# Adaptive average pooling in one dimension: the final scaling moves from ScalarE to GpSimd

## The chip, the cores and the metric

The kernel runs on one core of a Trainium2 chip. The metric is the device time of one execution in microseconds; the time before is the median of three runs. The engines are named as the profile names them: DVE (VectorE), ACT (ScalarE), POOL (GpSimd), PE (TensorE, unused here) and SP (SyncE, which issues the DMAs here). SPq and POOLq are the instruction queues of SP and POOL.

## What is computed

The input x is float32 of shape 32 x 256 x 4096. Each row of 4096 values is cut into 256 windows of 16, and the output is the mean of each window:

```python
for i in range(output_size):            # output_size = 256
    start = int(i * length / output_size)
    end = int((i + 1) * length / output_size)
    result[:, :, i] = np.mean(x[:, :, start:end], axis=-1)
```

134.2 MB are read and 8.4 MB are written; there is one addition for each value read.

## The kernel before

The 32 x 256 = 8192 rows are worked through in 16 tiles of 512 rows, four rows (R) on each of the 128 partitions. A tile `xin` thus has 1024 cells (windows) of 16 values per partition, 8.39 MB in all. The pool `inpool` has two buffers, so tile t + 2 can be loaded when tile t has been read for the last time.

For each tile, in this order in the text:

- SP issues the load (line 74).
- POOL takes the second half of the cells (512 of 1024) and adds the last eight values of each window onto the first eight, in place (line 77). That is an operation of 4096 elements per partition with two inputs.
- DVE sums the 16 values of each cell of the first half into the result (line 82, 8192 elements per partition), and needs only the load for it.
- DVE sums the eight remaining values of each cell of the second half (line 85, 4096 elements per partition), and waits for POOL's add.
- ACT multiplies the tile's 1024 results by 1/16, in place (line 88), and waits for line 85.

The results stay in the core's memory: those of the first 14 tiles in `res_many`, those of the last two in `res_few`. They leave in two stores, which SP issues as well through the function `store` (its DMA is line 61): `res_many` (7.34 MB) is issued once the last load has been issued, in the loop's last turn, and waits for the scaling of tile 13; `res_few` (1.05 MB) is issued after the loop and waits for the scaling of tile 15. Both stores wait in SP's queue in the order of the text, so a load that stands ahead of them is issued first.

Tile, the layer in which the kernel is written, sets the semaphores between the engines; each engine runs its instructions in the order of the text. At the end line 97 and what follows join the engines, and SP waits until both stores have landed (line 99). Line 116 stands for a preamble that fills four constants on POOL; line 130 for the entry into the program.

Of the kernel before, what the change touches and what calls it, by code (L numbers as in the profile page):

```python
# [1 line left out]

# [4 lines left out]


@with_exitstack
def kernel(  # L10
    ctx: ExitStack,
    tc: tile.TileContext,
    x: bass.AP,
    output_size: int,
    out: bass.AP,
):

    nc = tc.nc
    F32 = mybir.dt.float32
    X = mybir.AxisListType.X

    batch, channels, length = x.shape
    ob, oc, olen = out.shape
    assert ob == batch and oc == channels and olen == output_size
    assert length % output_size == 0
    window = length // output_size  # L30
    hw = window // 2
    inv_w = 1.0 / float(window)

    P = nc.NUM_PARTITIONS
    R = 4
    tail = 2
    rows = batch * channels
    assert rows % (P * R) == 0
    ntiles = rows // (P * R)
    head = ntiles - tail  # L40
    many = head * R
    few = tail * R
    cells = R * output_size
    m = cells // 2
    cols = R * length

    xr = x.rearrange("b c l -> (b c) l")
    orow = out.rearrange("b c o -> (b c) o")
    x_many = xr[0 : P * many, :].rearrange("(p r) l -> p (r l)", p=P, r=many)
    o_many = orow[0 : P * many, :].rearrange("(p r) o -> p (r o)", p=P, r=many)  # L50
    x_few = xr[P * many :, :].rearrange("(p r) l -> p (r l)", p=P, r=few)
    o_few = orow[P * many :, :].rearrange("(p r) o -> p (r o)", p=P, r=few)

    res_many = nc.alloc_sbuf_tensor("res_many", [P, head * cells], F32, align_bytes=256)
    res_few = nc.alloc_sbuf_tensor("res_few", [P, tail * cells], F32, align_bytes=256)
    inpool = ctx.enter_context(tc.tile_pool(name="inpool", bufs=2))

    stored = nc.alloc_semaphore("stored")

    def store(out, in_):  # L60
        ins = nc.sync.dma_start(out=out, in_=in_)
        tc.no_tile_sem_insts.add(ins.ins.name)
        ins.then_inc(stored, 16)

    for t in range(ntiles):
        k = t - head
        xin = inpool.tile([P, cells, window], F32, name="xin")
        if k < 0:
            res, base = res_many, t * cells
            src = x_many[:, t * cols : (t + 1) * cols]  # L70
        else:
            res, base = res_few, k * cells
            src = x_few[:, k * cols : (k + 1) * cols]
        nc.sync.dma_start(out=xin.rearrange("p o w -> p (o w)"), in_=src)  # L74
        if t == ntiles - 1:
            store(o_many, res_many[:, :])
        nc.gpsimd.tensor_add(  # L77
            out=xin[:, m:cells, 0:hw],
            in0=xin[:, m:cells, 0:hw],
            in1=xin[:, m:cells, hw:window],  # L80
        )
        nc.vector.reduce_sum(  # L82
            out=res[:, base : base + m], in_=xin[:, 0:m, :], axis=X
        )
        nc.vector.reduce_sum(  # L85
            out=res[:, base + m : base + cells], in_=xin[:, m:cells, 0:hw], axis=X
        )
        nc.scalar.mul(  # L88
            out=res[:, base : base + cells],
            in_=res[:, base : base + cells],  # L90
            mul=inv_w,
        )
    store(o_few, res_few[:, :])

    ctx.pop_all().close()
    tc.close()
    tc.compile()  # L97
    nc.sync.wait_ge(stored, 32)
    nc.sync.sem_clear(stored)


# [1 line left out]
_INS = ['x', 'output_size']  # L103
_OUTS = [((32, 256, 256), 'float32')]

_NUMBERS = {'output_size': 256}


# [26 lines left out]
```

## Time and profile before

| | |
|---|---|
| median of three runs | 333.5 us (333.26 to 333.58) |
| profiled execution | 333.14 us, of which the span in the profile 331.8 us |
| DVE busy | 209.7 us, 63% of the span, 32 instructions |
| POOL busy | 139.7 us, 42%, 20 instructions |
| ACT busy | 18.2 us, 5%, 17 instructions (16 scalings of 1.056 us, one table load of 1.283 us) |
| POOL's add, line 77 | 16 of 8.717 us |
| DVE's sums, lines 82 and 85 | 16 of 8.686 us and 16 of 4.420 us |
| DMA | 142.61 MB, mean 430 GB/s |

The span runs from the first to the last thing that the profile shows of the program. Busy times are those of instructions at work, without waits. In the profile's lists an operation reads "engine line operation output<-input (partitions x elements)". In the timeline the first column is the start in microseconds from the span's start, the second the duration, and the brackets hold how long the engine had been idle and what ended that. In lists of waits, "a <- b: total, times, longest" says that a waited for b.

### The profile page before, as it was taken

How to read it: one execution, taken by the hardware profiler on the slowest of the kernel's cores; microseconds unless marked ns; L12 is line 12 of the kernel's file. 1: busy time of each engine (PE TensorE's matmuls, PEld its weight loads, DVE VectorE, ACT ScalarE, POOL GpSimd, SP SyncE). 2: the span in 40 equal slices, each digit the busy share in tenths (PEclk: the TensorE clock that was granted, in tenths of full speed). 3: DMA queues.
4: the chain of work that ended last, by engine and by line, in shares of the span. 5: the costliest groups of instructions: out<-in, count | busy, mean ns of one | idle time of the engine just before them, and what ended most of it. 6: DMA issues, size and time to landing. Idle time of an engine off the chain costs nothing.

```text
span 331.8 us, 159 instructions
## 1 busy us (share of the span) xinstructions
DVE 209.7 (63%) x32; ACT 18.2 (5%) x17; POOL 139.7 (42%) x20
## 2 busy tenths in 40 slices
DVE  0029396692939669392966939295693929569392
ACT  1000101001010100001010000101000010100001
POOL 0027090642709164270906437090643709063370
DMA  9898989989898998989899898989899898989998
GB/s 379 379 506 379 506 379 411 474 379 506 379 506 379 427 458 379 506 379 506 379 458 427 379 506 379 506 379 498 387 403 482 379 506 379 506 379 442 411 442 348
DMA packets 2592, 142.61 MB, mean 430 GB/s; under 512 B 288, under 2 KB 288, under 8 KB 288
## 3 DMA queue, kind: packets, MB, share of 16 engines
q1 hardware_dynamic: 2592, 142.61, 99.4%
HBM read 134.22 MB, written 8.39 MB: 430 GB/s over the span
## 4 chain that ended last, share of the span: by engine, by line
DMA 66%; POOL 18%; DVE 11%; POOLq 3%; issue 0%; ACT 0%; SPq 0%
DMA xin<-in_x_dram 66%; POOL xin L77 18%; DVE res_many L85 9%; POOLq L97 3%; DVE res_few L85 1%; ACT res_few L88 0%; SPq L74 0%; POOLq L77 0%
## 5 line engine op out<-in xcount | busy, mean ns | idle before, releaser
L77 POOL TENSOR_TENSOR xin<-xin 128x4096 f32<-128x4096 f32 x16 | 139.5, 8717 | 181.4 <-DMA xin<-in_x_dram 181.4
L82 DVE TENSOR_REDUCE res_many<-xin 128x512 f32<-128x8192 f32 x14 | 121.6, 8686 | 101.3 <-DMA xin<-in_x_dram 101.3
L85 DVE TENSOR_REDUCE res_many<-xin 128x512 f32<-128x4096 f32 x14 | 61.9, 4420 | 2.3 <-POOL xin L77 2.1
L88 ACT ACTIVATE res_many<-res_many 128x1024 f32<-128x1024 f32 x14 | 14.8, 1056 | 271.3 <-DVE res_many L85 271.3
L82 DVE TENSOR_REDUCE res_few<-xin 128x512 f32<-128x8192 f32 x2 | 17.4, 8686 | 12.1 <-DMA xin<-in_x_dram 12.1
L85 DVE TENSOR_REDUCE res_few<-xin 128x512 f32<-128x4096 f32 x2 | 8.8, 4420 | 0.3 <-POOL xin L77 0.3
L88 ACT ACTIVATE res_few<-res_few 128x1024 f32<-128x1024 f32 x2 | 2.1, 1056 | 36.6 <-DVE res_few L85 36.6
L88 ACT ACT_TABLE_LOAD x1 | 1.3, 1283 | 0.7 <-PEq L116 0.7
L116 POOL MEMSET const-float32-0.0<- 128x1 f32 x1 | 0.1, 98 | 0.2 <-issue 0.2
L116 POOL MEMSET const-uint8-127<- 128x1 uint8 x1 | 0.1, 102 | 0.0
L116 POOL MEMSET const-bfloat16-1.0<- 128x1 bf16 x1 | 0.1, 101 | 0.0
L116 POOL MEMSET const-float32-1.0<- 128x1 f32 x1 | 0.1, 99 | 0.0
## 6 DMA issues: line engine op xcount, KB each, us to landing
out_dram<-res_many SPq DMA_DIRECT2D x1, 7168.0 KB, 41.2
out_dram<-res_few SPq DMA_DIRECT2D x1, 1024.0 KB, 4.9
xin<-in_x_dram SPq DMA_DIRECT2D x16, 25.4
```

What stands on the lines that cost most here:

```text
L77: nc.gpsimd.tensor_add(out=xin[:, m:cells, 0:hw], in0=xin[:, m:cells, 0:hw], in1=xin[:, m:cells, hw:window],)
L82: nc.vector.reduce_sum(out=res[:, base : base + m], in_=xin[:, 0:m, :], axis=X)
L85: nc.vector.reduce_sum(out=res[:, base + m : base + cells], in_=xin[:, m:cells, 0:hw], axis=X)
L88: nc.scalar.mul(out=res[:, base : base + cells], in_=res[:, base : base + cells], mul=inv_w,)
L97: tc.compile()
L116: nc = _bacc.Bacc("TRN2", target_bir_lowering=False, num_devices=1)
```

## The change

POOL multiplies each tile's 1024 results by 1/16 instead of ACT. The operation, its operands and its place in the text stay the same. ACT is left with no instruction of the kernel, and the table load ahead of its first one goes too.

```diff
-        nc.scalar.mul(
+        nc.gpsimd.tensor_scalar_mul(
             out=res[:, base : base + cells],
-            in_=res[:, base : base + cells],
-            mul=inv_w,
+            in0=res[:, base : base + cells],
+            scalar1=inv_w,
         )
```

In the built program POOL's instructions then stand in the order add (tile 0), scale (0), add (1), scale (1) and so on; those of DVE and SP stand as before. The two stores wait for POOL where they waited for ACT, and from the third tile on the add waits for its load and for POOL's own scaling two tiles before, where it waited for its load and for DVE.

## The prediction

> **What bounds the kernel now.** I read the page's slices and queue table first, then the timeline of the last tiles, then the waits of the DMA queue's own engine, and last the tail in windows of 0.1 us. The slices and the queue table:
>
> ```profile
> DMA  9898989989898998989899898989899898989998
> ...
> q1 hardware_dynamic: 2592, 142.61, 99.4%
> HBM read 134.22 MB, written 8.39 MB: 430 GB/s over the span
> ```
>
> One queue is at work for 99.4% of 16 engines' span, and no slice is below eight tenths. All traffic (16 loads of 8.39 MB, stores of 7.34 and 1.05 MB) goes through it one after the other. The timeline of the last two tiles, SP's issues among the engines' work:
>
> ```profile
> 282.64 4.42 DVE L85 TENSOR_REDUCE res_many<-xin 128x512 f32<-128x4096 f32 x1 [0.17 <-POOL xin L77]
> 287.09 0.33 SPq L74 DMA_DIRECT2D xin<-in_x_dram  x1
> 287.10 1.06 ACT L88 ACTIVATE res_many<-res_many 128x1024 f32<-128x1024 f32 x1 [18.23 <-DVE res_many L85]
> 288.18 0.35 SPq L61 DMA_DIRECT2D out_dram<-res_many  x1
> 293.09 8.69 DVE L82 TENSOR_REDUCE res_few<-xin 128x512 f32<-128x8192 f32 x1 [6.03 <-DMA xin<-in_x_dram]
> 293.20 8.72 POOL L77 TENSOR_TENSOR xin<-xin 128x4096 f32<-128x4096 f32 x1 [10.59 <-DMA xin<-in_x_dram]
> ...
> 312.47 8.69 DVE L82 TENSOR_REDUCE res_few<-xin 128x512 f32<-128x8192 f32 x1 [6.10 <-DMA xin<-in_x_dram]
> 312.58 8.72 POOL L77 TENSOR_TENSOR xin<-xin 128x4096 f32<-128x4096 f32 x1 [10.66 <-DMA xin<-in_x_dram]
> 321.33 4.42 DVE L85 TENSOR_REDUCE res_few<-xin 128x512 f32<-128x4096 f32 x1 [0.17 <-POOL xin L77]
> 325.78 1.06 ACT L88 ACTIVATE res_few<-res_few 128x1024 f32<-128x1024 f32 x1 [18.32 <-DVE res_few L85]
> 326.86 0.34 SPq L61 DMA_DIRECT2D out_dram<-res_few  x1
> ```
>
> A tile takes 312.47 - 293.09 = 19.38 us, and its bytes need that: 8.39 MB / 19.38 us = 433 GB/s. Its buffer is free when L85 ends (287.06); SP hands over the load after next at 287.09, while the load in flight lands only at 293.08. So 6.0 us of transfer are queued at each handover, and the queue does not run dry. The queue's own waits say which engine SP depends on:
>
> ```profile
> SPq L74 <- DVE res_many L85: 185.8, 14, 13.3
> ...
> SPq L61 <- ACT res_few L88: 38.3, 1, 38.3
> SPq L61 <- ACT res_many L88: 0.7, 1, 0.7
> ```
>
> The loads wait for DVE and for earlier loads; the scaling is awaited by the two stores alone. The chain of waits gives DMA 66%, POOL 18% and DVE 11%, but it follows each buffer's reuse and does not see that the other buffer's load runs meanwhile, so I do not price by it. What remains is the tail, where a store seems to wait for the last scaling. In windows of 0.1 us (bounds, length, busy time of DVE, ACT and POOL, clock, DMA share, GB/s):
>
> ```profile
> 326.50:326.60 0.10, 0.00 (x0) 0.10 (x1) 0.00 (x0) 1.00 3.97 1720
> ...
> 326.80:326.90 0.10, 0.00 (x0) 0.04 (x1) 0.00 (x0) 1.00 1.32 573
> 326.90:327.00 0.10, 0.00 (x0) 0.00 (x0) 0.00 (x0) 1.00 0.00 0
> ...
> 328.60:328.70 0.10, 0.00 (x0) 0.00 (x0) 0.00 (x0) 1.00 0.60 246
> ```
>
> A packet is counted whole where it starts: shares above 1 show it, and so does the first load, issued at 0.74, whose 65 KB packets already appear from 1.70 on. So the last 16 packets of the big store (57 KB each) start at 326.5 to 326.9. The row of 326.50 holds three of them with 3.97 x 0.1 us x 16 engines / 3 = 2.12 us each: the engines are busy until 328.62 to 329.0. The first packet of the small store starts at 328.6. The end is thus set by bytes too, and the last scaling has some cover.
>
> **The change part by part.** Removed: ACT's table load (1.28 us, 0.74 to 2.02) and 16 scalings of 1.056 us. ACT's first scaling starts at 35.75, so nothing waits for the table; cost of the removal 0, hidden by the first load. The instruction order of the changed build has POOL alternate add and scale, with DVE's and SP's instructions as before; the stores now wait for POOL.
>
> Added: 16 scalings of 128x1024 on POOL, an operation that the trace does not show there. Nearest rows: POOL's four start-up fills of one element take 0.10 us, which I take as the fixed cost; the add takes 8.717 us for 4096 outputs, (8717 - 100) / 4096 = 2.10 ns per element with two reads and a write. The scaling has one read and one write. High bound: it goes at the add's rate, 0.10 + 1024 x 2.10 ns = 2.25 us. Low bound: the add's time is its three streams in turn, and the scaling overlaps its two: a third of it, 0.10 + 0.72 = 0.82 us. I take 1.2 us (half the add's rate, 0.10 + 1.08, the reads in turn), which is near DVE's one-input rate (4420 / 4096 = 1.08 ns per element) and ACT's (1.03).
>
> The Trainium skill ("GPSIMD Engine Reference", 4.1 Engine selection, and 3.1) advises against elementwise work on GpSimd, as about twice as slow as VectorE for two inputs, but calls one input roughly line rate, and gives 1.03 cycles per element for the lightest loops; the add here agrees with its two-input figure of 2.6 cycles at 1.2 GHz (8717 ns / 4096 x 1.2 = 2.55). By that page the scaling is 1024 x 1.03 / 1.2 = 0.88 us, an estimate, and the sum below stays as it is.
>
> Where POOL starts after a signal: for the same landing it starts 0.11 us after DVE (312.58 against 312.47), so the scaling starts 0 to 0.11 us later than ACT's did.
>
> In the steady state: the next add is now queued on POOL behind the scaling, which waits for L85. For tile 13 the scaling would run from about 287.2 to 288.4; the add behind it starts at 293.20, when its load lands. So 4.8 us are spare (3.8 at 2.25 us). Behind the add stand L85 of the next tile and, behind that, SP's load; they are late only if the scaling takes over 6.0 us. The adds' wait for DVE becomes one for POOL's own scaling of two tiles before, long done. DVE idles while POOL scales, so no overlap of the two is added; cost 0. Were the cover gone, it would be the scaling's 1.2 us for each of 15 tiles, 18 us.
>
> The big store's issue moves from 288.18 to about 288.4 (289.5 at the high bound), but its first packet starts at 311.7, behind the load handed over at 287.09: 22 us of cover, cost 0.
>
> The tail: the last scaling starts at 325.78 to 325.89 and ends at 327.07 (chosen), so the small store is issued at 327.09 instead of 326.86, 0.23 us later (bounds: 0.24 earlier, 1.30 later). From issue to first packet the first load took 0.96 us, eleven of its 16 packets started by 1.36 us, and the last at 2.06 us. Issued at 326.86, the small store could have begun at 327.8 to 328.2, and the engines came free from 328.6: cover of 0.4 to 0.8 us, by the slowest packets none. The chosen 0.23 us lies inside: cost 0. At the high bound 1.30 - (0.4 to 0.8) = 0.5 to 0.9 us show; without cover 1.3 us. An earlier issue gains nothing, as the bytes ahead of it stay.
>
> **The sum:** 331.8 us span + 0, and 333.14 - 331.8 = 1.34 us around it: 333.14 us. The profiled execution is 0.36 below the median of the runs, 333.5, so I give 333.5.
>
> **The rivals.**
> (1) *The last scaling sticks out of the cover*: it costs as much per element as the add. For: POOL's only wide operation runs at that rate. Against: it has one read fewer. Time 333.5 + 0.5 to 0.9 = 334.0 to 334.4.
> (2) *Slower: a scaling that is slow by itself*, say at twice the add's rate, 4.4 us. It ends at 330.3, the small store's packets start 0.96 to 1.36 us later, at 331.2 to 331.6 instead of 328.6: 2.6 to 3.0 us, 336.1 to 336.5. It decides from about 2.3 us on, where the tail's loss passes 0.67 us. For: the operation's price on POOL is not in the trace. Against: no row of any engine is that slow per element.
> (3) *POOL becomes the bound*: a scaling over 5.9 us makes add, reduce and scaling longer than the 19.38 us of a load. At 8.7 us a tile takes 8.7 + 4.4 + 8.7 + 0.3 = 22.1 us, and from 22.55 on 16 of them end at 376; with store and launch about 382. It needs four times the add's rate.
> (4) *Faster: the table load held up the start.* It runs at 0.74 to 2.02, and five of the 16 first packets start at 2.2 to 2.8, after eleven by 2.1. Were these five released, up to 0.7 us would go: 332.8 to 333.3. Against: the late packets are shorter (2.8 us against 3.1), and the rate over all later windows is 437 GB/s whatever the stagger.
>
> **How the numbers follow.** Forecast (hidden) 0.60; (1) 0.17; (2) 0.11; (3) 0.03; (4) 0.09. A measurement of this kernel can tell about 0.2% (0.67 us) from no change. Of (1) a third passes it, of (4) half. Slower: 0.05 + 0.11 + 0.03 = 0.19. Faster: 0.05. Same: 0.76. The range: the forecast and the spread of the runs (333.26 to 333.58), down to 332.9 for most of (4), and up to 335.0, which holds (1), its case without cover (334.8), and the start of (2): about 0.87 of the chance.
>
> **What would show it.** POOL rows of line 88, 128x1024, near 1.2 us; the adds still released by the load and not by POOL's queue; SP's store of the small result released by POOL at about 327.1; its first packets still near 328.6, and no gap after the big store's last ones; tiles still 19.38 us apart. I am wrong if the scaling takes over 2.3 us, if the small store's packets start more than 0.7 us later than before, or if the tiles' spacing moves. If the first packets bunch by 2.1 us with the table load gone and the whole tail comes earlier, (4) is right.

## The result, and the profile after

The changed kernel takes 334.14 us (median of 10 runs, 333.82 to 334.6) against 333.4 us (10 runs, 333.26 to 333.58) for the kernel before: a ratio of 1.0024, 95% interval 1.0015 to 1.0032, so it is 0.7 us slower. The profiled execution took 334.06 us with a span of 332.6 us (before 333.14 and 331.8).

The page of the changed kernel, its queue table and POOL's groups (busy time and mean duration, then the idle time before and what ended it):

```profile
q1 hardware_dynamic: 2592, 142.61, 99.2%
...
L77 POOL TENSOR_TENSOR xin<-xin 128x4096 f32<-128x4096 f32 x16 | 139.5, 8717 | 71.9 <-DMA xin<-in_x_dram 71.9
L88 POOL TENSOR_SCALAR res_many<-res_many 128x1024 f32<-128x1024 f32 x14 | 38.7, 2768 | 63.6 <-DVE res_many L85 63.6
...
L88 POOL TENSOR_SCALAR res_few<-res_few 128x1024 f32<-128x1024 f32 x2 | 5.5, 2768 | 9.1 <-DVE res_few L85 9.1
```

The scaling takes 2.768 us on POOL, 2.6 times ACT's 1.056. The adds are as long as before and still end their waits on the load. The last two tiles in the changed kernel's timeline:

```profile
293.28 8.69 DVE L82 TENSOR_REDUCE res_few<-xin 128x512 f32<-128x8192 f32 x1 [6.09 <-DMA xin<-in_x_dram]
293.40 8.72 POOL L77 TENSOR_TENSOR xin<-xin 128x4096 f32<-128x4096 f32 x1 [3.35 <-DMA xin<-in_x_dram]
...
312.58 8.69 DVE L82 TENSOR_REDUCE res_few<-xin 128x512 f32<-128x8192 f32 x1 [6.02 <-DMA xin<-in_x_dram]
312.70 8.72 POOL L77 TENSOR_TENSOR xin<-xin 128x4096 f32<-128x4096 f32 x1 [3.28 <-DMA xin<-in_x_dram]
321.45 4.42 DVE L85 TENSOR_REDUCE res_few<-xin 128x512 f32<-128x4096 f32 x1 [0.18 <-POOL xin L77]
325.96 2.77 POOL L88 TENSOR_SCALAR res_few<-res_few 128x1024 f32<-128x1024 f32 x1 [4.54 <-DVE res_few L85]
328.75 0.34 SPq L61 DMA_DIRECT2D out_dram<-res_few  x1
```

Up to the last sum nothing has changed: the tiles are 312.58 - 293.28 = 19.30 us apart (19.38 before; over all tiles 19.32 and 19.33), POOL still idles 3.3 us before each of these adds, and tile 15 lands 0.11 us later than before. Then the last scaling runs to 328.73, and the small store is issued at 328.75 instead of 326.86. The tail in windows of 0.1 us (bounds, length, busy time of DVE and POOL, clock, DMA share, GB/s):

```profile
326.50:326.60 0.10, 0.00 (x0) 0.10 (x1) 1.00 3.97 1720
...
327.00:327.10 0.10, 0.00 (x0) 0.10 (x1) 1.00 2.65 1147
327.10:327.20 0.10, 0.00 (x0) 0.10 (x1) 1.00 0.00 0
...
329.50:329.60 0.10, 0.00 (x0) 0.00 (x0) 1.00 0.19 82
329.60:329.70 0.10, 0.00 (x0) 0.00 (x0) 1.00 2.30 983
```

The last packets of the big store start at 326.5 to 327.1 and take 2.12 us each, so the engines come free at 328.6 to 329.2. The small store's first packet starts at 329.5, where it started at 328.6 before. So the queue now runs dry for some 0.3 to 0.9 us, once, at the end.

### The profile page after: what moved, and what is told of

Read it like the earlier page. It is cut to its first block, busy times and chain, and to the rows that moved or that the text cites. A ratio compares the mean times of both kernels' runs of the same rounds, so it can differ in the third digit from the quotient of the medians.

```text
span 332.6 us, 158 instructions
## 1 busy us (share of the span) xinstructions
DVE 209.7 (63%) x32; POOL 183.9 (55%) x36
## 4 chain that ended last, share of the span: by engine, by line
DMA 66%; POOL 21%; DVE 9%; issue 2%; POOLq 1%; SPq 0%
DMA xin<-in_x_dram 66%; POOL xin L77 21%; DVE res_many L85 9%; POOLq L97 1%; SPq L74 0%; POOLq L77 0%
## 5 line engine op out<-in xcount | busy, mean ns | idle before, releaser
L88 POOL TENSOR_SCALAR res_many<-res_many 128x1024 f32<-128x1024 f32 x14 | 38.7, 2768 | 63.6 <-DVE res_many L85 63.6
L88 POOL TENSOR_SCALAR res_few<-res_few 128x1024 f32<-128x1024 f32 x2 | 5.5, 2768 | 9.1 <-DVE res_few L85 9.1
```

What stands on the lines that cost most here:

```text
L88: nc.gpsimd.tensor_scalar_mul(out=res[:, base : base + cells], in0=res[:, base : base + cells], scalar1=inv_w,)
```

## The experiments

Three theories were set against each other. A: only the last scaling costs, by what it sticks out of the cover that the big store's last packets give. B: POOL's scaling costs a little at every tile. C: the empty ACT or the missing table load changes the start (the first load landed at 22.76 instead of 22.50).

**Where the loss sits: the last tile alone.** In the first kernel POOL scales all tiles but the last, in the second the last alone:

```diff
+        if t == ntiles - 1:
+            nc.scalar.mul(...)
+        else:
             nc.gpsimd.tensor_scalar_mul(...)
```

> POOL scales tiles 0 to 14, ACT scales the last tile alone (its table load is back). Theory A (only the last scaling costs: it ends 1.9 us later and the last bytes of the big store cover about 1.0 us of that): the small store is issued near 327.0 again, its first packet at about 328.6, time within 0.2 us of the kernel before. Rival B (the scaling on POOL costs a little at every tile, by its traffic or by a later add): about 15/16 of the loss stays, 0.7 us above the kernel before.

Measured: 333.48 us against 333.36, ratio 1.0003 (0.9994 to 1.0012): no loss that can be told. In its timeline the store's issue is back at 1.11 us after the last sum's end at 326.02, as before:

```profile
326.05 1.06 ACT L89 ACTIVATE res_few<-res_few 128x1024 f32<-128x1024 f32 x1 [324.06 <-DVE res_few L85]
327.13 0.34 SPq L61 DMA_DIRECT2D out_dram<-res_few  x1
```

The counterpart, with the two calls exchanged:

> ACT scales tiles 0 to 14, POOL the last tile alone. Theory A: the whole loss is here, 0.6 to 0.9 us above the kernel before; the small store issued near 328.7, first packet near 329.5. Rival B: within 0.1 us of the kernel before. Rival C (the missing table load or an empty ACT changes the start, where the first load landed at 22.76 instead of 22.50): within 0.3 us of the kernel before, since ACT and its table load are there.

Measured: 334.07 us against 333.36, ratio 1.0018 (1.0009 to 1.0028). One scaling on POOL costs as much as sixteen; the other fifteen are free as far as these intervals can tell, as A says. B falls. C falls too: ACT and its table load are in this kernel, and so is the loss.

**How much the tail hides.** Extra multiplications by 1.0 of the last tile's results on ACT move the small store's issue and nothing else; a third kernel leaves the last scaling out:

```diff
         nc.scalar.mul(...)
+        if t == ntiles - 1:
+            nc.scalar.mul(out=..., in_=..., mul=1.0)   # once, or twice
```

> The kernel before, with the last tile's results multiplied once more on ACT, by 1.0: the small store is issued about 1.08 us later and nothing else changes. Theory A with a cover of about 1.0 us: 0 to 0.2 us above the kernel before, the small store's first packet at 328.6 to 328.8. Without a cover: 1.08 us above.

> The kernel before, with the last tile's results multiplied twice more on ACT, by 1.0: the small store is issued about 2.15 us later, a little more than POOL's scaling does. Theory A: 2.15 - 1.0 = 1.0 to 1.2 us above the kernel before, though POOL and the rest of ACT are as before. Rival B: within 0.2 us of the kernel before, as the cost would be POOL's.

> The kernel before without the scaling of the last tile, whose outputs stay sums instead of means: the small store is issued about 1.08 us earlier, near 325.8. Theory A: the bytes ahead of it set its start, so nothing is gained, within 0.2 us of the kernel before, first packet still near 328.6. If the last scaling was on the path of the kernel before: 1.0 us faster.

Measured, against 333.46 us for the kernel before: twice 333.45 (ratio 1.0, 0.9991 to 1.0009), thrice 334.52 (1.0032, 1.0021 to 1.0044), without 333.35 (0.9997, 0.9988 to 1.0006). The tail of the kernel that scales thrice, from its timeline:

```profile
321.40 4.42 DVE L85 TENSOR_REDUCE res_few<-xin 128x512 f32<-128x4096 f32 x1 [0.18 <-POOL xin L77]
325.85 1.06 ACT L88 ACTIVATE res_few<-res_few 128x1024 f32<-128x1024 f32 x1 [18.44 <-DVE res_few L85]
326.94 2.14 ACT L95 ACTIVATE res_few<-res_few 128x1024 f32<-128x1024 f32 x2
329.11 0.34 SPq L61 DMA_DIRECT2D out_dram<-res_few  x1
```

There is no scaling on POOL in it, and it loses more than the changed kernel, because its store is issued later still. The kernel that scales twice issues its store 1.09 us later than the kernel before, counted from the last sum's end, and loses nothing:

```profile
321.58 4.42 DVE L85 TENSOR_REDUCE res_few<-xin 128x512 f32<-128x4096 f32 x1 [0.18 <-POOL xin L77]
...
328.20 0.34 SPq L61 DMA_DIRECT2D out_dram<-res_few  x1
```

The lists of DMA issues give the time from the small store's issue to its landing, the end of the transfer (last column, us): without the last scaling, before, and with ACT scaling twice:

```profile
out_dram<-res_few SPq DMA_DIRECT2D x1, 1024.0 KB, 6.0
...
out_dram<-res_few SPq DMA_DIRECT2D x1, 1024.0 KB, 4.9
...
out_dram<-res_few SPq DMA_DIRECT2D x1, 1024.0 KB, 3.8
```

The runs in order of the delay (end of the last line 85 to the store's issue, both from the timelines; landing from the lists of DMA issues; time against the kernel before of the same runs):

| kernel | delay, us | issue to landing, us | time, us |
|---|---|---|---|
| no last scaling | 0.08 | 6.0 | -0.11 |
| before | 1.11 | 4.9 | 0 |
| POOL, last tile on ACT | 1.11 | 4.9 | +0.12 |
| ACT twice | 2.20 | 3.8 | -0.01 |
| POOL, the last tile alone | 2.89 | 3.8 | +0.71 |
| changed kernel | 2.88 | 3.8 | +0.74 |
| ACT thrice | 3.29 | 3.8 | +1.06 |

Up to a delay of 2.2 us the landing takes up what the issue loses: delay and landing together stay at 6.0 to 6.1 us, and so does the time. No landing in these runs is shorter than 3.8 us, so from a delay of 6.0 - 3.8 = 2.2 us on each microsecond of delay is one of time (2.88 - 2.2 = 0.68 and 3.29 - 2.2 = 1.09, against 0.74 and 1.06). This knee does not depend on the engine: ACT and POOL lie on the same line. One expectation was missed: with ACT scaling twice the small store's first packet starts at 329.0, not by 328.8, and no time is lost by it. The first packet's start alone therefore doesn't set the end; probably the engines that finish the big store last do, but no run separates the two.

**Less of the scaling behind the last sum.** All of it stays on POOL, but the last tile's first half is scaled right after line 82, while DVE still sums the second half:

```diff
+        if t == ntiles - 1:
+            nc.gpsimd.tensor_scalar_mul(out=res[:, base : base + m], ...)
         nc.vector.reduce_sum(...)            # second half
+        lo = base + m if t == ntiles - 1 else base
         nc.gpsimd.tensor_scalar_mul(
-            out=res[:, base : base + cells], ...)
+            out=res[:, lo : base + cells], ...)
```

> All scalings on POOL, ACT empty; the last tile's is cut in two, the first half of its results being scaled while DVE still sums the second. Theory A: what is left after the last sum is one scaling of 512 elements, about 1.4 us if the price goes with the elements; the store is issued 0.5 us later than in the kernel before, which the cover holds: within 0.2 us of the kernel before. Rivals B and C: the loss stays, 0.6 to 0.8 us above.

Measured: 333.62 us against 333.36, ratio 1.0005 (0.9996 to 1.0013). Its timeline:

```profile
321.55 1.49 POOL L86 TENSOR_SCALAR res_few<-res_few 128x512 f32<-128x512 f32 x1
326.00 1.49 POOL L95 TENSOR_SCALAR res_few<-res_few 128x512 f32<-128x512 f32 x1 [2.97 <-DVE res_few L91]
327.52 0.34 SPq L61 DMA_DIRECT2D out_dram<-res_few  x1
```

The delay is 327.52 - 325.92 = 1.60 us, inside the cover, and the landing takes 4.4 us, so it again ends 6.0 us after the last sum. Most of the loss is gone. The 0.26 us between the medians is a little more than the 0.2 us expected; whether it is a difference, the interval doesn't tell. ACT is empty here too, and the first load landed at 22.43, while in the six kernels with ACT at work it landed at 22.39 to 22.70: the late 22.76 of the changed kernel does not come from the empty ACT.

**What the scaling costs on POOL.** One kernel scales tile after tile in other sizes and forms:

> The price of the scaling on POOL, by tile: one of 1024 elements, 2 of 512, 4 of 256, 8 of 128, 16 of 64, a multiplication by a tensor of constants, a scaling into another buffer and a copy back, a scalar that is read from a tensor, two operations in one instruction, and one tile on DVE. If the price goes with the elements: 1.40, 0.72, 0.4 and 0.25 us for 512, 256, 128 and 64, with 0.1 us fixed. If it is mostly a fixed cost of starting the operation (1.7 us and 1.05 ns per element): 2.2 us for 512 and 1.8 us for 64. If working in place slows it: about 1.2 us into the other buffer. The multiplication by a tensor at the add's rate: 2.25 us, so less than the scaling though it reads twice as much. Time: no expectation, several tiles issue more.

Its groups by shape:

```profile
L96 POOL TENSOR_SCALAR res_many<-res_many 128x64 f32<-128x64 f32 x16 | 5.9, 371 | 2.0 <-DVE res_many L88 1.1
...
L96 POOL TENSOR_SCALAR res_many<-res_many 128x512 f32<-128x512 f32 x2 | 3.0, 1490 | 3.0 <-DVE res_many L88 3.0
L103 POOL TENSOR_SCALAR res_many<-res_many,cst 128x1024 f32<-128x1024 f32 x1 | 2.8, 2846 | 4.6 <-DVE res_many L88 4.6
L100 POOL TENSOR_SCALAR scr<-res_many 128x1024 f32<-128x1024 f32 x1 | 2.8, 2769 | 4.5 <-DVE res_many L88 4.5
L98 POOL TENSOR_TENSOR res_many<-res_many,cst 128x1024 f32<-128x1024 f32 x1 | 2.3, 2340 | 4.5 <-DVE res_many L88 4.5
L105 POOL TENSOR_SCALAR res_many<-res_many 128x1024 f32<-128x1024 f32 x1 | 1.0, 1049 | 4.5 <-DVE res_many L88 4.5
L101 POOL COPY res_many<-scr 128x1024 f32<-128x1024 f32 x1 | 1.0, 1037 | 0.1
```

Line 96 is the scaling in pieces, line 98 the multiplication by a tensor, line 100 the scaling into another buffer and 101 the copy back, line 103 the scalar read from a tensor, line 105 the two operations in one instruction. The price goes with the elements: (2769 - 1490) / 512 = 2.50 ns each, and 0.21 us fixed, twice the 0.1 us assumed. Working in place (line 100 writes elsewhere and takes as long) and the constant's source (line 103) do not explain it. Multiplying by a whole tensor of constants (line 98) is cheaper, though it reads twice as much. And line 105, two multiplications by 0.25 in one instruction, takes 1.049 us, as little as a copy. On DVE the same scaling takes 0.694 us. The kernel ran once, in 334.27 us; it ends with a scaling of 2.77 us, as the changed kernel does.

So the next kernel asked what makes that form cheap:

> What makes the scaling dear, by tile: one operation with 1/16 as before; two operations as (x 1/16, x 1.0), (x 1/16, + 0.0), (+ 0.0, x 1/16), (x 0.25, x 0.25); the two-operation form in 2, 4, 8 and 16 pieces; one addition of 0.0 alone; one multiplication by 0.25 alone; one multiplication with an explicit empty second operation. If the missing second operation is the cause: all two-operation forms near 1.05 us, all with one near 2.77 us, whatever the operation or constant. If the constant is the cause: the 0.25 forms near 1.05 us, those with 1/16 near 2.77 us. If the multiplication is: the addition alone near 1.05 us. Time: no expectation.

Its groups by shape, one line of each kind:

```profile
L107 POOL TENSOR_SCALAR res_many<-res_many 128x1024 f32<-128x1024 f32 x1 | 2.8, 2775 | 4.5 <-DVE res_many L85 4.5
L110 POOL TENSOR_SCALAR res_many<-res_many 128x1024 f32<-128x1024 f32 x1 | 2.8, 2775 | 4.5 <-DVE res_many L85 4.5
...
L113 POOL TENSOR_SCALAR res_many<-res_many 128x1024 f32<-128x1024 f32 x1 | 2.8, 2770 | 4.5 <-DVE res_many L85 4.5
...
L105 POOL TENSOR_SCALAR res_many<-res_many 128x512 f32<-128x512 f32 x2 | 1.2, 620 | 3.9 <-DVE res_many L85 3.8
L94 POOL TENSOR_SCALAR res_many<-res_many 128x1024 f32<-128x1024 f32 x1 | 1.0, 1049 | 4.5 <-DVE res_many L85 4.5
L96 POOL TENSOR_SCALAR res_many<-res_many 128x1024 f32<-128x1024 f32 x1 | 1.0, 1047 | 4.5 <-DVE res_many L85 4.5
L98 POOL TENSOR_SCALAR res_many<-res_many 128x1024 f32<-128x1024 f32 x1 | 1.0, 1046 | 4.5 <-DVE res_many L85 4.5
```

A single addition of 0.0 (line 107), a single multiplication by 0.25 (110) and one by 1/16 with an explicitly empty second operation (113) all take 2.77 us. Two operations, in whatever order and kind (94: x 1/16, x 1.0; 96: x 1/16, + 0.0; 98: + 0.0, x 1/16), take 1.05. Neither the constant nor the operation matters, only whether the second one is there: (1046 - 620) / 512 = 0.83 ns per element with it, 2.50 ns without. This kernel, which also ran once, ends with a two-operation scaling and took 333.35 us.

**The change with the cheap form.**

```diff
-        nc.gpsimd.tensor_scalar_mul(out=..., in0=..., scalar1=inv_w)
+        nc.gpsimd.tensor_scalar(out=..., in0=..., scalar1=inv_w, scalar2=1.0,
+                                op0=mult, op1=mult)
```

> The change as it is, but POOL's scaling is written with two operations in one instruction (times 1/16, times 1.0); ACT is empty. Theory A with the price of the two-operation form (1.05 us for 1024 elements, seen on one tile): the last scaling ends 0.1 us later than ACT's, the small store is issued near 327.0, its first packet at about 328.7 or when the big store's packets end, time within 0.1 us of the kernel before. If that one tile's price had another cause (its place, its constants): scalings near 2.77 us and 0.6 to 0.9 us above the kernel before.

Measured: 333.53 us against 333.49, ratio 1.0005 (0.9996 to 1.0014). Its timeline:

```profile
326.22 1.04 POOL L88 TENSOR_SCALAR res_few<-res_few 128x1024 f32<-128x1024 f32 x1 [4.54 <-DVE res_few L85]
327.29 0.34 SPq L61 DMA_DIRECT2D out_dram<-res_few  x1
```

The delay is 327.29 - 326.13 = 1.16 us, 0.05 more than with ACT, and no loss can be told any more, with POOL still doing all the scaling. None of these kernels is faster than the one before: the kernel without the last scaling shows that an earlier store gains nothing.

## Why the prediction was wrong

- *What bounds the kernel*: right. Loads and stores follow one another on the queue, the tiles' spacing did not move, and fifteen of the sixteen scalings cost nothing that can be told (last tile on ACT: ratio 1.0003). The big store's later issue (290.07 instead of 288.18) cost nothing either, as worked out.
- *The price of the scaling*: the step that failed. It was put at 1.2 us, with a high bound of 2.25 us from the add's rate, because the scaling has one read fewer. It measured 2.77 us, 0.5 us above the bound, and the prediction's own signs of being wrong came: a scaling over 2.3 us, and the small store's first packet 0.9 us later than before. The bound took POOL's time to grow with the number of streams; the runs show a one-operation scaling that is slower per element (2.50 ns) than the add with two inputs (2.10 ns). An operation that no row of the trace shows on that engine was bounded from above by another operation, and that was no bound. This step alone turns the forecast: with 2.77 us the prediction's own cover of 0.4 to 0.8 us leaves 2.88 - 1.11 - (0.4 to 0.8) = 1.0 to 1.4 us outside. What made it dear is a matter of form: with a second operation it takes 1.05 us, even less than the chosen value, and there the forecast of no change holds (ratio 1.0005).
- *The Trainium skill's rule*, "GPSIMD Engine Reference", 4.1 Engine selection, that one input goes at roughly line rate: here it holds for the copy (1.037 us for 1024 elements) and for the two-operation form (0.83 ns per element, by estimate one cycle at the 1.2 GHz of that page's 1. Specifications), and not for the one-operation form, three times as slow per element.
- *The tail*: the mechanism was right, the cover too small. 0.4 to 0.8 us were worked out from the first load's issue to its first packets (0.96 to 1.36 us). (The windows of the first load show twelve of its first 16 packets starting by 2.1 us, not eleven, and four later; the bounds stay.) The changed kernel's small store needs only 329.5 - 328.75 = about 0.8 us, and the runs put the knee at a delay of 2.2 us, so the cover is 2.2 - 1.11 = 1.1 us. With the measured price and cover the sum is: 2.88 - 1.11 - 1.1 = 0.67 us, against 0.74 measured.
- *The rivals*: the first named the right place, the last scaling outside the cover, and its time of 334.0 to 334.4 us holds the measured 334.14. That is luck: its price was 0.5 us too low and its cover 0.3 to 0.7 us too small, and the two errors largely cancel. The stated range of 332.9 to 335.0 us holds the measured time only because it was drawn wide enough for this rival; the forecast of no change itself was wrong. The second rival had the right cause, a scaling that is slow by itself, but put its price at 4.4 us; the argument against it, that no row of any engine is that slow per element, again judged an operation by the rows of others. POOL stayed far from being the bound (3.3 us idle before each add). The faster start of the fourth did not come: without the table load five of the first load's 16 packets still start at 2.1 to 2.7 us, and with POOL's cheap form, where the table load is gone too, the time is that of the kernel before.

## What to carry to other kernels

When work moves to another engine, its price there is unknown until a row of that engine shows that very form of the operation. Here another operation's rate gave no upper bound, and a second operation in the instruction made the scaling 2.6 times as fast (1.05 against 2.77 us). In a loop that the DMA queue bounds, look at the one place where the queue can run dry, the end: find when the engines come free from the bytes ahead, and count how late the last store may be issued. Here delays up to there were free, on ACT and on POOL alike, and beyond it they counted in full.

## What the runs showed of the hardware that was not expected

- On POOL, a tensor-scalar instruction with one operation takes 0.21 us + 2.50 ns per element of float32 on each partition, and one with two operations 0.19 us + 0.83 ns (from 512 and 1024 elements). Why the shorter form is the slower one, the runs do not show.
- The small store, issued 2.2 us or more after the last sum, needs 3.8 us from issue to landing for 1.05 MB, of which about 0.8 us pass before its first packet; both are the same in the four kernels of the table that issue it so late.
